# Expert weights with consecutive rows on each partition, in a two-block transformer kernel

## The chip, the cores and the metric

One NeuronCore of one Trainium2 chip runs the whole program; everything is float32 in DRAM. The metric is the device time of one execution in microseconds (us), given as the median of several runs. A profile of one execution stands beside it.

Engines are named as the profile names them: PE is the tensor engine's matmul, PEld its load of the stationary operand, DVE the vector engine, ACT the scalar engine, POOL the GpSimd engine, SP the sync engine, which here only issues DMAs. [...]

## The reference, cut to what matters

The program is two blocks of two layers each on 256 tokens of 1024 features (272 with the 16 meta tokens of block 1). The change touches only the mixture of experts that ends each layer of block 1, and a few vectors set up for it:

```python
def hier_moe(h, w_grp, b_grp, w_rtr, b_rtr, w1, w3, w2):
    t = h.reshape(-1, d)                       # [272, 1024]
    ...                                        # a group of experts, then two of its eight, and their gates
    hid = jax.nn.silu(jnp.einsum('td,edf->tef', t, w1)) * jnp.einsum('td,edf->tef', t, w3)
    y = jnp.einsum('tef,efd->td', hid * combine[..., None].astype(hid.dtype), w2)
```

There are 32 experts. `w1` and `w3` of one expert are [1024, 256], `w2` is [256, 1024]; each is 1 MB, so a layer reads 96 MB of expert weights. Each token uses two experts. `h` comes out of a layer norm with gain and bias `ln1_g`, `ln1_b`.

## The kernel before, in words

**Weights.** The contraction over 1024 features needs them on the 128 partitions in 8 blocks. The kernel puts feature `128 k + p` on partition `p` in block `k`: a weight of [1024, 256] is loaded as a tile [128, 8, 256] with `rearrange("(k p) n -> p k n")` (`moe_load`, L1109 to L1114), so that each partition receives eight separate rows of 1 KB. `w2` goes through `wrows` (L211 to L215) as [128, 2, 1024], two separate rows of 4 KB for each partition.

**Rings.** `w1` and `w3` of four experts, eight tiles `wb`, make one group; three rings hold them (5, 4 and 6 tiles: RB, RX, RC at L184), which is nearly two groups. `w2` of the four experts, tiles `w`, uses the general ring of four tiles (`wtile`, L200), which the memory projection's weights (`mem_kv`, L1595) share. All these loads are issued by SP from one queue in program order; a load waits there until its tile's last reader is done, and all loads behind it wait too.

**One group of experts** (the loop at L1253, eight groups for each of two layers): `onehot` makes a 0/1 matrix that puts each token into one of 32 slots of its expert (L1150). `gather` (L1179 to L1190) multiplies the normed tokens by it, block by block: the stationary operand is `y[t][:, k * 128:(k + 1) * 128]`, the moving one is the one-hot matrix, and the result, [128 features, 128 slots], gets the norm's gain and bias as per-partition columns of `K.lcol` (`gain`, L1171 to L1177: odd blocks on DVE, even ones on ACT) and becomes `hg[:, k, :]`. `up` (L1192) contracts `hg` with the weights, four experts side by side in four 32-column strips of the PE; tanh and two DVE products follow. `down` (L1205) transposes the hidden values by halves of 128 (L1208), multiplies by `w2` (L1216) and copies to `ysl`. `scatter` (L1221) sums the result into the token-major `acc`. Then the loads of the next group are named in program order.

A float32 matmul appears in the profile as two records, each with its own weight load. In layer 0 the tokens come in three tiles (128, 128 and 16 rows), so one gather has 8 x 3 x 2 = 48 weight loads of 128 columns; in layer 1 there are two tiles and 32 loads.

**Order of the work.** The order of instructions on each engine is set when the program is built, by a planner with costs of its own. In the first groups it puts `up(g)`, `gather(g+1)`, `down(g)`; from the fourth group on, `gather(g+1)` stands before or inside `up(g)`.

**Norm vectors.** `setup` loads `ln1_g`, `ln1_b` and other vectors as rows of 128 (L296 to L302), and `feature_columns` (L305) transposes them once into `K.lcol`, where column `16 i + 8 l + k` holds features `128 k + p`. `K.lcol` also serves the router (L674, L677) and the residual (`row_bank`, L328).

**Overflow.** `moe_overflow` (L1296) is a loop that runs only when an expert has more than 32 tokens; in the profiled execution none of its instructions stands (L1329 has no record).

Of the kernel before, what the change touches and what calls it, by code (L numbers as in the profile page):

```python
# [20 lines left out]
CAP = 32  # L21
# [19 lines left out]
def _consts():  # L41
    """Tables that depend on the shapes alone: masks, identities, rotary tables of block 1."""
# [64 lines left out]
def build(tc, A, out, dbg=None, stop=None):  # L107
    nc = tc.nc
    es = ExitStack()
    with es:  # L110
# [9 lines left out]
        # the memory's keys and values, and scratch, for the whole run  # L120
        K.pt = es.enter_context(tc.tile_pool(name="mem0", bufs=1, side="right"))
        K.mem = {0: mem_tiles(K, K.pt)}
        for l in range(2):
            with ExitStack() as st:
# [17 lines left out]
                # the expert weights start to come in beside the output projection  # L142
# [5 lines left out]
            with ExitStack() as st:  # L148
                # what dies first lies where the next phase starts
                K.pe = st.enter_context(tc.tile_pool(name="moee%d" % l, bufs=1))  # L150
                K.pf = st.enter_context(tc.tile_pool(name="moef%d" % l, bufs=1))
                K.wc = st.enter_context(tc.tile_pool(name="wringc%d" % l, bufs=RC))
                K.p = st.enter_context(tc.tile_pool(name="moe%d" % l, bufs=1))
                b1_moe(K, l)
# [12 lines left out]
        # block 2: what is needed first lies on the right, where the expert weights were  # L167
# [15 lines left out]
# tiles of the three rings of expert weights; up to which weight of a group the first two serve  # L183
# [20 lines left out]
def wcols(K, w, c0, n=256):  # L204
    """Columns c0.. of a [1024, N] weight as [128, 8, n]."""
    t = wtile(K)[:, :8 * n].rearrange("p (k n) -> p k n", n=n)
    K.nc.sync.dma_start(t, w.rearrange("(k p) n -> p k n", p=128)[:, :, c0:c0 + n])
    return t


def wrows(K, w, r0, nk=2):  # L211
    """Rows r0.. of a [K, 1024] weight as [128, nk, 1024]."""
# [5 lines left out]
def split(K, x, shape, pool=None):  # L218
    """A float32 weight block of up to 1024 columns as an exact sum of two float32r blocks."""
# [17 lines left out]
def mm3(K, out, a, b, start, stop):  # L237
    """out += a^T b to float32 accuracy; a and b are (high, low) pairs."""
# [6 lines left out]
def put(K, dst, src, sl):  # L245
    """Writes src (PSUM or SBUF) as a high and a low part."""
# [14 lines left out]
def setup(K):  # L261
# [23 lines left out]
    # the convolutions' taps as columns  # L285
# [4 lines left out]
    # a_log, dt_bias on all partitions  # L290
# [14 lines left out]
def feature_columns(K):  # L305
    """The other vectors over features as columns."""
# [5 lines left out]
    K.dng = K.const.tile([128, 2], F32, name="dng")  # L312
    V.tensor_scalar(K.dng, K.lcol[:, 64:66], 0.5, None, op0=OP.mult)


def to_T(K, src, t):
    """One token-major tile -> feature-major high and low parts."""
# [10 lines left out]
def row_bank(K, k, tag):  # L328
    """512 features from column k of K.lcol on, along a row that is the same on all partitions."""
# [6 lines left out]
def interleave(gens):  # L336
    """Runs generators in turn, one step of each, until all are done."""
# [9 lines left out]
def yield_from(gen):  # L347
    """Runs a generator to its end and gives what it returns."""
# [7 lines left out]
def b1_attention(K, l, mix, st):  # L356
# [55 lines left out]
    # small columns: db, da, iw  # L412
# [147 lines left out]
    # the memory of block 2 and the first expert weights come in early  # L560
# [13 lines left out]
def b1_sparse_meta(K, sqT, skT, vtok, mix):  # L574
    """The 16 meta tokens, all heads at once."""
# [85 lines left out]
def router_weights(K, l, p):  # L661
    """Router weights with the norm's gain on them, high and low parts; the norm's bias goes with theirs."""
# [19 lines left out]
def b1_project(K, l, mix):  # L682
    """Output projection, residual, layer norm, router logits and choices."""
# [30 lines left out]
    def norm(t, halves):  # L714
        """Residual and norm before gain and bias (left in K.y); feature-major parts of it for the router."""
# [67 lines left out]
def norm_stats(K, y, P, ss, junk, at=0):  # L783
    """Minus the mean and the inverse deviation of y [P, 1024] into ss[:, 2] and ss[:, 5]; ss[:, 0:2] holds the half sums."""
# [16 lines left out]
class Route:  # L801
    """Grouped top-2 routing, one token tile after the other: the expert slots of the tokens and their gates."""
# [26 lines left out]
    def choose(self, t):  # L829
        """The two experts of each token."""  # L830
# [18 lines left out]
    def rank(self, t):  # L849
        """The token's rank among those of the expert."""  # L850
# [9 lines left out]
    def gates(self, t):  # L860
        """Half of the gates of a token tile."""
# [16 lines left out]
class Delta:  # L878
    """Gated delta rule on one token tile: two chunks of 64, or the 16 meta tokens."""
# [12 lines left out]
    def pre(self):  # L892
# [42 lines left out]
        # normalised keys and queries, feature-major  # L935
# [33 lines left out]
        # T = (1 + L)^-1 by block doubling; U its transpose  # L969
# [37 lines left out]
        # token-major keys and values  # L1007
# [101 lines left out]
def moe_load(K, l, g, n):  # L1109
    """Weight n of a group of four experts: w1 of each, then w3 of each."""  # L1110
    t = (K.wb if n < NB else K.wx if n < NX else K.wc).tile([128, 8, 256], F32, name="wb", tag="wb")
    w = K.A["w1" if n < 4 else "w3"][l, 4 * g + n % 4]
    K.nc.sync.dma_start(t, w.rearrange("(k p) n -> p k n", p=128))
# [8 lines left out]
def b1_moe(K, l):  # L1122
    """Tokens are gathered into CAP slots per expert; tokens past the slots of an expert take a dense path in a loop
    that only runs when an expert has any."""
# [8 lines left out]
    def load(g):  # L1133
        w = [[moe_load(K, l, g, 4 * i + j) for j in range(4)] for i in range(2)]
        return w, [wrows(K, w2[4 * g + j], 0) for j in range(4)]

    # the first group's loads began beside the projection
# [4 lines left out]
    w2t = [wrows(K, w2[j], 0) for j in range(4)]  # L1142
# [4 lines left out]
    def onehot(g):  # L1147
        """Token -> slot of a group's experts."""
# [5 lines left out]
    def gates(g, oh):  # L1154
        """The gates there."""
# [4 lines left out]
    def gated(og_):  # L1160
        """Gated slot -> token."""
# [9 lines left out]
    def gain(dst, src, k):  # L1171
        """The first norm's gain and bias of feature block k."""
        g, b = (K.lcol[:, 16 * i + 8 * l + k:16 * i + 8 * l + k + 1] for i in range(2))
# [5 lines left out]
    def gather(oh):  # L1179
        hg = K.pe.tile([128, 8, 128], F32, name="hg")  # L1180
        for kk in range(2):
            ps = bank(K)
            for k in range(4 * kk, 4 * kk + 4):
                for i, t in enumerate(seq):
                    P = TP[t]
                    PE.matmul(ps[:, (k % 4) * 128:(k % 4) * 128 + 128], y[t][:P, k * 128:(k + 1) * 128],  # L1186
                              oh[:P, t, :], start=(i == 0), stop=(i == nt - 1))
# [17 lines left out]
    def down(th, w2t):  # L1205
        ps = bank(K)
        for j in range(2):
            PE.transpose(ps[:, j * 128:j * 128 + 128], th[:, j * 128:j * 128 + 128], ident)  # L1208
# [29 lines left out]
    # the meta tokens' sums lie beside them  # L1238
# [3 lines left out]
    def init():  # L1242
        """The residual, of the normed tokens."""
# [30 lines left out]
    # tokens without a slot  # L1274
# [21 lines left out]
def moe_overflow(K, l, ovf, acc, rows, tiles, gain):  # L1296
    """Adds the contribution of the tokens that found no slot, whatever their number."""
# [3 lines left out]
    with tc.If(n > 0):  # L1301
        # tokens feature-major, and the gates of those past the slots
        yT = [K.wx.tile([128, 8, TP[t]], F32, name="yT%d" % t, tag="wb") for t in tiles]
        for t in tiles:
            P = TP[t]
            for b in range(2):
                ps = bank(K)
                for j in range(4):
                    k = 4 * b + j
                    PE.transpose(ps[:, j * P:(j + 1) * P], K.y[t][:P, k * 128:(k + 1) * 128], c["ident"][:P, :P])  # L1310
# [3 lines left out]
        with tc.For_i(0, 32, 1) as e:  # L1314
            def cols(w):
                t = wtile(K).rearrange("p (k n) -> p k n", n=256)
                nc.sync.dma_start(t, w[l, bass.ds(e, 1)].rearrange("o (k p) n -> p (o k) n", p=128))
# [3 lines left out]
            nc.sync.dma_start(w2t, A["w2"][l, bass.ds(e, 1)].rearrange("o (k p) n -> p (o k) n", p=128))  # L1321
            for t in tiles:
# [13 lines left out]
                for j in range(2):  # L1336
                    PE.transpose(ps[:, j * 128:j * 128 + P], th[:P, j * 128:j * 128 + 128], c["ident"][:P, :P])
# [10 lines left out]
def setup2(K):  # L1348
    """Per-feature vectors of block 2."""
# [30 lines left out]
def setup2_rest(K):  # L1380
    """Masks, gains on token-major heads, and rotary tables."""
# [10 lines left out]
    # cos and sin of positions * inv, with the multiples of 2 pi taken off exactly  # L1392
# [29 lines left out]
def rms_T(K, src, gain, dst):  # L1422
    """RMS norm of two token-major tiles, feature-major as high and low parts [128, 8, 256]; gain is columns [128, 8]."""
# [23 lines left out]
def rstd_heads(K, ss, P, n, d):  # L1447
    """(ss / d + 1e-6) ** -0.5 on [P, n]."""
# [25 lines left out]
def weave(a, b, na, nb):  # L1474
    """Runs generator a beside b: nb steps of b for every na of a."""
    done = [False, False]
    i = 0
# [776 lines left out]
```

## Time and profile before

| | |
|---|---|
| median of 3 runs | 2196.48 us (2181.83 to 2199.58) |
| span of the profiled execution, first to last instruction | 2178.1 us |
| mean granted PE clock | 0.954 |
| PE busy | 2037.9 us, 94% of the span |
| DMA traffic from HBM | 411.5 MB, 190 GB/s on average |
| expert stage of layer 0 | about 316 to 585 us |
| expert stage of layer 1 | about 886 to 1139 us |

The span is that of one execution of its own, and each run is timed from outside; the runs lie 4 to 21 us above this span. A busy PE is not a PE at its peak, since the ends of its matmuls are modelled. The stages are read from the first gather matmul to the last scatter matmul of each layer.

### The profile page before, as it was taken

How to read it: one execution, taken by the hardware profiler on the slowest of the kernel's cores; microseconds unless marked ns; L12 is line 12 of the kernel's file. 1: busy time of each engine (PE TensorE's matmuls, PEld its weight loads, DVE VectorE, ACT ScalarE, POOL GpSimd, SP SyncE). 2: the span in 40 equal slices, each digit the busy share in tenths (PEclk: the TensorE clock that was granted, in tenths of full speed). 3: DMA queues.
4: the chain of work that ended last, by engine and by line, in shares of the span. 5: the costliest groups of instructions: out<-in, count | busy, mean ns of one | idle time of the engine just before them, and what ended most of it. 6: DMA issues, size and time to landing. Idle time of an engine off the chain costs nothing. (4 is left out here: it accounts for less than half of the span.)

```text
span 2178.1 us, 34809 instructions
## 1 busy us (share of the span) xinstructions
PE 2037.9 (94%) x14216; PEld 1588.2 (73%) x14216; DVE 1091.5 (50%) x2179; ACT 762.0 (35%) x1478; POOL 358.9 (16%) x342
## 2 busy tenths in 40 slices
PE   8999999999699999988768999999999999999999
PEld 7888665544299887543326779889878869898987
DVE  6658444221376583521116674555545575555554
ACT  5214322111242243211015434455534524445543
POOL 1325000000022430000001130123400031122410
PEclk9999799999899997999889899999999989999999
DMA  7304288999942154999995243254555434244553
GB/s 220 97 20 136 78 290 297 340 356 371 301 132 74 44 187 141 344 368 366 365 335 170 83 166 120 88 184 155 173 194 163 133 116 146 88 153 145 168 193 116
DMA packets 321670, 414.90 MB, mean 190 GB/s; under 512 B 25480, under 2 KB 277970, under 8 KB 321506
## 3 DMA queue, kind: packets, MB, share of 16 engines
q1 hardware_dynamic: 315110, 410.85, 56.4%
q8 instruction: 114, 1.87, 0.4%
q10 hardware_dynamic: 6396, 1.77, 0.3%
q14 instruction: 50, 0.41, 0.1%
HBM read 411.54 MB, written 1.05 MB: 189 GB/s over the span
## 5 line engine op out<-in xcount | busy, mean ns | idle before, releaser
L233 DVE TENSOR_TENSOR wl<-w,wh 128x1024 fp32r<-128x1024 f32 x329 | 411.5, 1253 | 270.8 <-ACT wh L232 263.5
L232 ACT CAST wh<-w 128x1024 fp32r<-128x1024 f32 x350 | 365.7, 1047 | 429.8 <-PE ps_d L241 251.3
L240 PE MATMUL ps_d<-hh,wh 128*128 128x256 f32 (+1 forms) x1632 | 481.7, 296 | 5.5 <-ACT tg L2161 1.9
L242 PE MATMUL ps_d<-hh,wl 128*128 128x256 f32 (+1 forms) x1632 | 475.1, 291 | 0.3
L241 PE MATMUL ps_d<-hl,wh 128*128 128x256 f32 (+1 forms) x1632 | 475.0, 291 | 0.0
L240 PEld LDWEIGHTS ps_d<-hh,wh 128*128 128x128 f32 x1632 | 310.1, 190 | 17.4 <-issue 6.4
L242 PEld LDWEIGHTS ps_d<-hh,wl 128*128 128x128 f32 x1632 | 310.6, 190 | 9.1 <-DVE wl L233 6.9
L241 PEld LDWEIGHTS ps_d<-hl,wh 128*128 128x128 f32 x1632 | 310.1, 190 | 4.7 <-issue 0.8
L1197 PE MATMUL ps_d<-wb,hg 128*32 128x256 f32 x2048 | 156.0, 408 | 33.1 <-DMA wb<-in_w 33.0
L1197 PEld LDWEIGHTS ps_d<-wb,hg 128*32 128x32 f32 x2048 | 73.4, 117 | 106.5 <-DMA wb<-in_w 43.4
L2221 POOL TENSOR_TENSOR relu<-relu 128x256 f32<-128x256 f32 x64 | 86.6, 1354 | 129.6 <-ACT relu L2220 129.6
L1186 PE MATMUL ps_c<-oh,y 128*128 128x128 f32 (+1 forms) x640 | 101.9, 297 | 0.0
L1201 DVE SCALAR_TENSOR_TENSOR mth<-mth,ps_d 128x256 f32<-128x256 f32 x16 | 6.7, 421 | 183.5 <-ACT mth L1200 183.4
L1186 PEld LDWEIGHTS ps_c<-oh,y 128*128 128x128 f32 (+1 forms) x640 | 82.7, 189 | 21.1 <-issue 5.7
L1216 PE MATMUL ps_d<-w,hid 128*32 128x512 f32 x512 | 80.9, 637 | 12.1 <-ACT hid L1210 7.9
L795 POOL TENSOR_TENSOR lnst<-lnst,nhalf 128x1 f32<-128x1 f32 (+1 forms) x5 | 4.9, 980 | 479.7 <-DVE lnst L794 477.8
L1228 DVE TENSOR_TENSOR yacc<-yacc,ps_c 128x512 f32<-128x512 f32 x56 | 38.5, 687 | 83.6 <-PE ps_c L1225 83.6
L1200 ACT ACTIVATE mth<-ps_d 128x256 f32<-128x256 f32 x16 | 6.1, 383 | 211.5 <-PE ps_d L1197 211.5
L233 POOL TENSOR_TENSOR wl<-w,wh 128x1024 fp32r<-128x1024 f32 x21 | 50.0, 2383 | 129.2 <-ACT wh L232 119.8
L2175 POOL TENSOR_TENSOR mergedT<-mergedT,tg 128x256 f32<-128x256 f32 x32 | 32.6, 1041 | 234.0 <-DVE tg L2173 234.0
L1216 PEld LDWEIGHTS ps_d<-w,hid 128*32 128x32 f32 x512 | 21.7, 115 | 60.3 <-issue 36.8
L1225 PE MATMUL ps_c<-ysl,ohT 128*128 128x512 f32 (+1 forms) x140 | 64.5, 603 | 0.0
(679 smaller groups left out, 3686.1 us busy)
## 6 DMA issues: line engine op xcount, KB each, us to landing
wb<-in_w SPq DMA_DIRECT2D x128, 1024.0 KB, 12.0
w<-in_w_in SPq DMA_DIRECT2D x82, 1024.0 KB, 5.3
w<-in_w SPq DMA_DIRECT2D x64, 1024.0 KB, 11.4
w<-in_w_up SPq DMA_DIRECT2D x32, 1024.0 KB, 5.3
w<-in_w_down SPq DMA_DIRECT2D x32, 1024.0 KB, 4.9
w<-in_w_out SPq DMA_DIRECT2D x16, 1024.0 KB, 4.8
w<-in_w_branch SPq DMA_DIRECT2D x24, 512.0 KB, 4.2
w<-in_mem_w_kv SPq DMA_DIRECT2D x8, 1024.0 KB, 5.7
```

The source lines that it names most:

```text
L232: K.nc.scalar.copy(h, x)
L233: eng.tensor_tensor(lo, x, h.bitcast(F32), op=OP.subtract)
L240: PE.matmul(out, a[0], b[0], start=start, stop=False, skip_group_check=True)
L241: PE.matmul(out, a[0], b[1], start=False, stop=False, skip_group_check=True)
L242: return PE.matmul(out, a[1], b[0], start=False, stop=stop, skip_group_check=True)
L1186: PE.matmul(ps[:, (k % 4) * 128:(k % 4) * 128 + 128], y[t][:P, k * 128:(k + 1) * 128], oh[:P, t, :], start=(i == 0), stop=(i == nt - 1))
L1197: PE.matmul(pu[j * 32:j * 32 + 32, i * 256:i * 256 + 256], hg[:, k, j * 32:j * 32 + 32], wts[i][j][:, k, :], start=(k == 0 and i == 0), st ...
L1216: PE.matmul(ps[q * 32:q * 32 + 32, :], hid[:, j, q * 32:q * 32 + 32], w2t[q][:, j, hf * 512:(hf + 1) * 512], start=(j == 0), stop=(j == 1) ...
L1225: PE.matmul(ps[rows[t]], ohT[:, off:off + P], ysl[:, hf * 512:(hf + 1) * 512], start=True, stop=True)
L1228: V.tensor_tensor(sl, sl, ps[rows[t]], op=OP.add)
L2175: G.tensor_tensor(m, m, tg, op=OP.add)
L2221: G.tensor_tensor(r, r, r, op=OP.mult)
```

## The change

The expert weights are loaded so that a partition holds consecutive rows: features `8 p + k` for `w1` and `w3`, hidden features `2 p + j` for `w2`. The rest follows that order: `gather` takes every eighth column of the token tile as its stationary operand, the transposes in `down` every second column of the hidden values, and the norm's gain and bias come from a new tile `K.gcol` that is loaded by two DMAs on ACT's queue. The residual and the router keep `K.lcol`. The overflow loop is changed the same way. The diff also removes comments and docstrings, which are left out here.

```diff
 def feature_columns(K):
...
     K.dng = K.const.tile([128, 2], F32, name="dng")
+    K.gcol = K.const.tile([128, 2, 2, 8], F32, name="gcol")
+    for i, nm in enumerate(("ln1_g", "ln1_b")):
+        K.nc.scalar.dma_start(K.gcol[:, i], K.A[nm].rearrange("l (p k) -> p l k", k=8))
     V.tensor_scalar(K.dng, K.lcol[:, 64:66], 0.5, None, op0=OP.mult)
...
 def moe_load(K, l, g, n):
     t = (K.wb if n < NB else K.wx if n < NX else K.wc).tile([128, 8, 256], F32, name="wb", tag="wb")
     w = K.A["w1" if n < 4 else "w3"][l, 4 * g + n % 4]
-    K.nc.sync.dma_start(t, w.rearrange("(k p) n -> p k n", p=128))
+    K.nc.sync.dma_start(t, w.rearrange("(p k) n -> p k n", k=8))
+    return t
+
+
+def moe_load2(K, w):
+    t = wtile(K).rearrange("p (k n) -> p k n", n=1024)
+    K.nc.sync.dma_start(t, w.rearrange("(p k) n -> p k n", k=2))
     return t
...
-        return w, [wrows(K, w2[4 * g + j], 0) for j in range(4)]
+        return w, [moe_load2(K, w2[4 * g + j]) for j in range(4)]
...
-    w2t = [wrows(K, w2[j], 0) for j in range(4)]
+    w2t = [moe_load2(K, w2[j]) for j in range(4)]
...
     def gain(dst, src, k):
-        g, b = (K.lcol[:, 16 * i + 8 * l + k:16 * i + 8 * l + k + 1] for i in range(2))
+        g, b = (K.gcol[:, i, l, k:k + 1] for i in range(2))
...
-                    PE.matmul(ps[:, (k % 4) * 128:(k % 4) * 128 + 128], y[t][:P, k * 128:(k + 1) * 128],
-                              oh[:P, t, :], start=(i == 0), stop=(i == nt - 1))
+                    PE.matmul(ps[:, (k % 4) * 128:(k % 4) * 128 + 128], y[t][:P, k::8], oh[:P, t, :], start=(i == 0), stop=(i == nt - 1))
...
-            PE.transpose(ps[:, j * 128:j * 128 + 128], th[:, j * 128:j * 128 + 128], ident)
+            PE.transpose(ps[:, j * 128:j * 128 + 128], th[:, j::2], ident)
```

## Rows read from the trace of the kernel before

**Rows 1.** The page: busy time and instructions of each engine, then 40 equal slices.
```profile
PE 2037.9 (94%) x14216; PEld 1588.2 (73%) x14216; DVE 1091.5 (50%) x2179; ACT 762.0 (35%) x1478; POOL 358.9 (16%) x342
...
GB/s 220 97 20 136 78 290 297 340 356 371 301 132 74 44 187 141 344 368 366 365 335 170 83 166 120 88 184 155 173 194 163 133 116 146 88 153 145 168 193 116
```

**Rows 2.** Windows in the expert stages: first from:to and length; then stretches of one load kind.
```profile
core 0: us, PE busy (x) PEld busy (x) DVE busy (x) ACT busy (x) POOL busy (x), PEclk, DMA share, GB/s
480.00:536.00 56.00, 52.88 (x416) 27.84 (x416) 12.00 (x22) 5.74 (x14) 0.00 (x0) 0.97 1.08 366
536.00:580.00 44.00, 32.90 (x216) 11.19 (x216) 6.88 (x15) 4.77 (x11) 0.00 (x0) 0.88 0.99 344
...
1085.00:1131.00 46.00, 32.28 (x243) 12.57 (x247) 6.05 (x14) 4.57 (x11) 0.00 (x0) 0.80 1.06 375
395.00:410.00 15.00, 14.41 (x78) 6.88 (x78) 5.61 (x11) 3.26 (x7) 0.00 (x0) 1.00 1.10 348
1120.00:1130.00 10.00, 7.47 (x65) 3.31 (x68) 1.16 (x4) 0.76 (x2) 0.00 (x0) 0.67 1.03 409
```

**Rows 3.** DMA packets in 395 to 410, then in 1120 to 1130.
```profile
DMA packets 5177, 5.22 MB, mean 348 GB/s; under 512 B 80, under 2 KB 5177, under 8 KB 5177
...
DMA packets 1068, 4.09 MB, mean 409 GB/s; under 512 B 69, under 2 KB 69, under 8 KB 1068
```

**Rows 4.** Waits of PE in 316 to 580, in 886 to 1131, in 886 to 1019.
```profile
PE ps_d L1197 <- DMA wb<-in_w: 7.7, 4, 2.4
...
PE ps_d L1197 <- DMA wb<-in_w: 25.3, 13, 2.5
...
PE ps_d L1216 <- DMA w<-in_w: 3.5, 5, 0.9
...
PE ps_d L1197 <- DMA wb<-in_w: 4.4, 2, 2.4
...
PE ps_d L1216 <- DMA w<-in_w: 1.6, 2, 0.9
```

**Rows 5.** Timeline of PE: start, length, line, operation, count, idle time before.
```profile
355.52 0.62 PE L1197 MATMUL ps_d<-wb,hg 128*32 128x256 f32 x2
...
382.05 0.62 PE L1197 MATMUL ps_d<-wb,hg 128*32 128x256 f32 x2
...
553.55 3.65 PE L1197 MATMUL ps_d<-wb,hg 128*32 128x256 f32 x60 [1.07 <-DMA wb<-in_w]
...
565.58 5.92 PE L1197 MATMUL ps_d<-wb,hg 128*32 128x256 f32 x58 [1.93 <-DMA wb<-in_w]
...
904.76 3.74 PE L1186 MATMUL ps_c<-oh,y 128*128 128x128 f32 x32
```

**Rows 6.** Weight loads of the gather and of `up`: ns min/median/max, first and last start.
```profile
L1186 PEld LDWEIGHTS ps_c<-oh,y x640: 181/192/192, 316.2 to 1074.0; 128*128 128x128 f32 x128, 16*128 16x128 f32 x32
...
L1197 PEld LDWEIGHTS ps_d<-wb,hg x2048: 106/110/178, 325.2 to 1126.7; 128*32 128x32 f32 x187
```

**Rows 7.** Two DVE lines of block 2, the same view: ns min/median/max.
```profile
L1914 DVE TENSOR_TENSOR raw<-R,fcol x8: 569/598/1580, 1226.9 to 1746.4; 128x240 f32<-128x240 f32 x8
...
L1797 DVE TENSOR_TENSOR garg<-G x12: 407/418/428, 1230.1 to 1763.7; 128x256 f32<-128x256 f32 x12
```

**Rows 8.** SP in layer 1: its timeline, a wait of it, and loads issued from 1019 on.
```profile
1007.88 11.10 SPq L214 DMA_DIRECT2D w<-in_w  x4
...
SPq L214 <- PE ps_p L1600: 6.3, 1, 6.3
...
wb<-in_w SPq DMA_DIRECT2D x24, 1024.0 KB, 12.0
w<-in_w SPq DMA_DIRECT2D x12, 1024.0 KB, 14.4
```

**Rows 9.** DMA in 1152.2 to 1160: packets, and one of the loads.
```profile
DMA packets 2591, 1.71 MB, mean 219 GB/s; under 512 B 1695, under 2 KB 2032, under 8 KB 2590
...
qkg<-in_nsa_k_norm SPq DMA_DIRECT2D x2, 96.0 KB
```

More of the change, by code (lines that the diff above doesn't have):

```diff
@@ L1309, in moe_overflow @@
                     k = 4 * b + j
-                    PE.transpose(ps[:, j * P:(j + 1) * P], K.y[t][:P, k * 128:(k + 1) * 128], c["ident"][:P, :P])
+                    PE.transpose(ps[:, j * P:(j + 1) * P], K.y[t][:P, k::8], c["ident"][:P, :P])
                 for j in range(4):
@@ L1316, in cols @@
                 t = wtile(K).rearrange("p (k n) -> p k n", n=256)
-                nc.sync.dma_start(t, w[l, bass.ds(e, 1)].rearrange("o (k p) n -> p (o k) n", p=128))
+                nc.sync.dma_start(t, w[l, bass.ds(e, 1)].rearrange("o (p k) n -> p (o k) n", k=8))
                 return t
@@ L1320, in moe_overflow @@
             w2t = wtile(K).rearrange("p (k n) -> p k n", n=1024)
-            nc.sync.dma_start(w2t, A["w2"][l, bass.ds(e, 1)].rearrange("o (k p) n -> p (o k) n", p=128))
+            nc.sync.dma_start(w2t, A["w2"][l, bass.ds(e, 1)].rearrange("o (p k) n -> p (o k) n", k=2))
             for t in tiles:
@@ L1336, in moe_overflow @@
                 for j in range(2):
-                    PE.transpose(ps[:, j * 128:j * 128 + P], th[:P, j * 128:j * 128 + 128], c["ident"][:P, :P])
+                    PE.transpose(ps[:, j * 128:j * 128 + P], th[:P, j::2], c["ident"][:P, :P])
                 hid = K.pe.tile([128, 2, 128], F32, name="hid")
```

## The prediction, made before the changed kernel was run

> **What bounds the kernel now.** I read the page first. PE is busy for 94% of the span, but the share of busy time is a mean, and the slices of GB/s show two stretches, about 270 to 600 us and 870 to 1140 us, in which the traffic stays between 290 and 371 GB/s while elsewhere it is mostly under 200 [rows 1]. They are the two expert stages. Nothing outside them is changed, so the next view is the windows inside them: the DMA engines' share is 0.99 to 1.08, so they have no free time, and PE is busy for 52.88 of 56 us in 480 to 536, but only for 32.9 of 44 us in 536 to 580 and for 32.28 of 46 us in 1085 to 1131 [rows 2]. Both resources are close to the bound, PE ahead in layer 0 and DMA in layer 1. PE's waits say by how much: in layer 0's stage PE waits 7.7 us for `wb`; in layer 1's it waits 25.3 + 3.5 = 28.8 us for expert weights, 4.4 + 1.6 = 6.0 us of them before 1019 [rows 4]. All that a faster load can give back is in these waits and in the slow clock behind them.
>
> **The loads.** In a stretch with `w1`/`w3` alone DMA moves 348 GB/s, with `w2` alone 409 [rows 2]; the packets are 1 KB in the first (5.22 MB in about 5,100) and 4 KB in the second (4.09 MB in about 1,000 over 2 KB), one for each row on each partition [rows 3]. One MB (1.0486e6 bytes) takes 3.01 us in the one form and 2.56 us in the other. The difference, 0.45 us for 768 packets less on 16 engines, is 9.4 ns a packet. With 8 KB on a partition the packets fall from 256 to 128, so 2.56 - 8 x 0.0094 = 2.49 us, some 421 GB/s; no row shows packets of 8 KB, and the bounds are 2.56 (no faster than 4 KB) and 2.49. I take 2.49: 0.52 us less for a `w1`/`w3` tile, 0.07 for a `w2` tile, so 8 x 0.52 + 4 x 0.07 = 4.4 us for a group, 71 us for all 16, if all of it were on the path. That the two inner dimensions are joined to one run is shown by a load elsewhere: the `qkg` rows, written in the program as 3 x 64 elements, move 96 KB to 128 partitions; in their window 2032 - 1695 = 337 packets have between 512 B and 2 KB [rows 9], where only 768 B rows and one load with 128 rows of 512 B can stand.
>
> [...]
>
> **The gather's weight loads.** This is the price. The stationary operand becomes `y[:, k::8]`, one float32 in every 32 bytes. The trace has no stationary operand with such a step, so I bound it. A load of 128 columns lasts 192 ns, one of 32 columns 110 ns [rows 6]: 82 ns for 96 columns, 0.85 ns a column, 109 ns for the 128. In layer 1 a gather's 32 loads with their matmuls take 3.74 us, 117 ns each [rows 5], so loads are about as long as what they hide behind, and a longer load shows in full. The lower bound is no extra at all: a gain is excluded, since the same columns pass either way. For the upper side the nearest rows are two on DVE. L1914 reads float32 at the same step of 32 bytes: 569 ns at best for 240 elements; L1797 reads 256 elements at a step of 8 bytes or less in 418 ns [rows 7]. At about 1 ns an element 240 would take 401, so the step costs 168 ns, 0.70 ns an element (by the median, 197 ns or 0.82). For 128 columns that is 90 to 105 ns, close to a doubled load (109). I take 100 ns a load, being nearest to the only rows with this step; the ends kept for the range are 0 and, for a load four times as long, 327.
>
> [...]
>
> In numbers: 8 gathers x 48 loads x 0.1 = 38.4 us in layer 0 and 8 x 32 x 0.1 = 25.6 us in layer 1.
>
> **What of it is on the path.** Layer 0: between 355.52 and 382.05 one group takes 26.5 us on PE [rows 5], with no DMA wait, and until about 536 PE is the one that is late. So the 38.4 us lie on PE's chain. Given back are the 7.7 us of waits for `wb` and the slow clock after them: 58 matmuls of `up` took 5.92 us behind the waits against 3.65 for 60 [rows 5], 2.3 us. After that DMA has slack, since its group takes 12 x 2.49 = 30 us against PE's 26.5 + 4.8 = 31.3. Layer 0: 38.4 - 10.0 = +28.4.
>
> Layer 1: SP's queue is held at 1007.88 for 11.10 us, 6.3 of them by the memory projection's matmuls on PE, which occupy two of the four `w` tiles; behind this stand 24 `wb` and 12 `w` loads [rows 8], which are DMA's path to the end of the stage. The hold moves with PE: six gathers lie before it, 6 x 3.2 = 19.2 us, less the 6.0 us of waits. Behind it the loads are faster by 24 x 0.52 + 12 x 0.07 = 13.3 us. Sum 19.2 - 6.0 - 13.3 = -0.1; the two gathers after it (6.4 us) fit into the 22.8 - 13.3 = 9.5 us of waits that are left. Layer 1: 0. What is late next there is PE and DMA alike.
>
> The rest I cost at nothing. The transposes' loads are 32 in all at a step of 8 bytes, which L1797 reads without a loss; were each doubled it would be about 3 us. `K.gcol` adds two small DMAs on ACT's queue, issued with the constants some 250 us before the first gather; ACT is busy 35% of the span, and its issue delays nothing that PE waits for then. SP's queue gets no more entries than before.
>
> **Sum.** +28.4 - 0.1 = +28, less a little for a planner that may put the gather back behind `up`, where the wait for tanh is covered: +27 us on a span of 2178.1. Set on the median of the runs, 2196.5, that is **2223.5 us**, 1.2% slower.
>
> **The rivals.**
> (B) *Strided loads cost PE nothing.* Then layer 0 keeps the -10.0 and layer 1 has -6.0 - 13.3 = -19.3 and some 3 us of slow clock (0.80 granted in 1085 to 1131, between the two levels [rows 2]). Sum -32: 2164 us, 1.5% faster. For it: a PE load takes 0.85 ns a column, slower than its matmuls stream, and its read path need not be DVE's. Against it: rows 7. It decides below 20 ns a load, where faster loads outweigh what is left.
> (C) *The strided load takes four times as long*, 327 ns more for 640 loads: 209 us, less some 39 given back: 2366 us. Nothing in the trace speaks for it, but nothing shows the step on PE.
> (D) *The runs are not joined, or 8 KB runs are no faster* than what is there. Then only the price is left: 38.4 - 10.0 and, in layer 1, 19.2 - 6.0 = 13 before the hold: 2238 us. Against it: rows 9 and the step from 348 to 409.
> (E) *A price in between* (about 50 ns a load): 14 - 10 in layer 0 and -6 - 13 + 10 in layer 1, some -4: 2192 us.
>
> **How the numbers follow.** Chances: forecast 0.52, B 0.33, C 0.06, D 0.06, E 0.03. The forecast's own range is +10 to +42: below if the planner moves the gathers or the price is 85 ns, above if it is 109 or the waits come back elsewhere. The whole range goes from B's better half (2152) to the forecast's upper end (2240); left out are C, a part of D and the tails, about 0.17. About 1% (22 us) is what a measurement can tell from no change. Faster by more: B, 0.33. Slower by more: 0.6 of the forecast (0.31), C and two thirds of D, 0.41. Within 1%: 0.26.
>
> **What would show it.** Right: the weight loads of the gather's line near 290 ns where they were 192, a gather of layer 1 in about 7 us for 3.74; packets of 8 KB, and over 410 GB/s in stretches with `wb` alone; PE's waits for `wb` in layer 0 gone, its stage about 28 us longer, layer 1's as long as before. Wrong: loads at 192 ns with layer 1's stage 20 us shorter (B), packets of 1 KB (D), or an order of `up` and gather that differs from before by more than the loads explain.

## The result, and the profile after

The changed kernel takes 2252.44 us (2244.98 to 2266.49, 4 runs), the kernel before in the same measurement 2191.97 us; the ratio is 1.029, 95% interval 1.024 to 1.034. The forecast said slower, 2223.5 us; the measured time lies 12 us above the upper end of its range. The direction is that of the forecast, and so is the first cause, the strided weight load. The size is not: 60 us for 27. A second cause, a fall of PE's granted clock in layer 0's stage (0.97 before, 0.79 after), stood in no term of the sum.

The page of the changed kernel, with the rows that answer to [rows 1], and the granted clock in the same 40 slices:
```profile
PE 2156.3 (95%) x14216; PEld 1697.3 (75%) x14216; DVE 1092.4 (48%) x2179; ACT 761.7 (34%) x1478; POOL 358.9 (16%) x342
...
PEclk9999598678789997799998989999999989999999
...
GB/s 217 88 30 165 30 279 238 266 234 357 272 291 86 57 100 143 189 334 351 354 424 261 133 123 135 88 145 149 171 195 175 140 112 139 85 142 153 173 191 114
```
The number of PE instructions is the same, but PE is busy for 118 us more and PEld for 109 us more. The granted clock is a share of full speed; every clock record of these two traces is 1.00 or 0.50, the upper and the lower level of what follows, and a figure between them is a mean over a window. In the first expert stage (slices 7 to 12) the granted clock is at 0.6 to 0.8, where [rows 2] had 0.88 to 1.00, and the traffic lies between 234 and 357 GB/s: DMA waits there for PE to free its tiles (in layer 0's stage SP waits 126 us for the matmuls of `up`, 38 us before). One slice of layer 1's stage shows 424 GB/s.

The weight loads of the gather (line 1198, line 1186 before) and of `up` (line 1208), to be held against [rows 6]: ns min/median/max.
```profile
L1198 PEld LDWEIGHTS ps_c<-oh,y x640: 307/334/340, 327.9 to 1163.7; 128*128 128x128 f32 x128, 16*128 16x128 f32 x32
...
L1208 PEld LDWEIGHTS ps_d<-wb,hg x2048: 106/110/178, 344.1 to 1201.1; 128*32 128x32 f32 x187
```
The load of the gather went from 192 to 334 ns; the load of `up`, which was not touched, is at 110 ns as before.

The timeline of PE, first in layer 0, then in layer 1, as in [rows 5]:
```profile
410.51 5.77 PE L1227 MATMUL ps_d<-w,hid 128*32 128x512 f32 x32 [0.46 <-ACT hid L1221]
...
429.11 16.22 PE L1198 MATMUL ps_c<-oh,y 128*128 128x128 f32 x48
...
1011.09 7.78 PE L1198 MATMUL ps_c<-oh,y 128*128 128x128 f32 x32
...
1019.68 3.64 PE L1227 MATMUL ps_d<-w,hid 128*32 128x512 f32 x32 [0.59 <-ACT hid L1221]
```
A gather of layer 1 takes 7.78 us for 3.74. One of layer 0 takes 16.22; before, the same 48 matmuls stood in one row of the timeline with 8.71 us. The first row is a product with `w2` that stands about 1 us behind the gather before that one: 5.77 us, where the same 32 matmuls take 3.64 in layer 1; the granted clock of this stretch was 0.62.

The windows of a gather, the first row from the kernel before (391 to 400, layer 0):
```profile
391.29:399.92 8.63, 8.63 (x50) 6.69 (x50) 2.22 (x5) 1.30 (x3) 0.00 (x0) 1.00 1.10 349
```
and from the changed kernel, two in layer 0, one in layer 1, then a stretch of 33 us with expert weights alone:
```profile
429.11:445.08 15.97, 15.97 (x49) 12.71 (x49) 2.22 (x5) 1.30 (x3) 0.00 (x0) 0.59 1.01 423
562.13:570.32 8.19, 8.19 (x25) 6.35 (x24) 0.00 (x0) 0.00 (x0) 0.00 (x0) 0.50 0.46 192
1011.09:1018.67 7.58, 7.58 (x34) 7.58 (x33) 1.88 (x5) 1.84 (x4) 0.00 (x0) 1.00 1.01 426
1127.00:1160.00 33.00, 30.84 (x221) 19.78 (x221) 5.64 (x12) 4.13 (x10) 0.00 (x0) 0.95 1.01 424
```
The DMA view of that stretch, as in [rows 3]:
```profile
DMA packets 1923, 13.98 MB, mean 424 GB/s; under 512 B 219, under 2 KB 219, under 8 KB 219
```
The columns after the length are the busy times of PE, PEld, DVE, ACT and POOL, then the granted clock. Read PEld against the length. In layer 1 a load is under way all the time (7.58 of 7.58). In layer 0 it is so for 12.71 of 15.97 us; the other 3.26 us are the 16 places in a gather where the operand changes between 128 and 16 rows, 0.20 us each on average. Before, this gap was (8.63 - 6.69) / 16 = 0.12 us. The clock is the other difference: 1.00 in layer 1 and before, 0.59 and 0.50 in the changed kernel's layer 0.

The two differences are one. The fifth gather of layer 0 stands in two pieces, at two levels of the clock:
```profile
457.56:463.12 5.56, 5.56 (x19) 4.78 (x18) 0.56 (x1) 0.39 (x1) 0.00 (x0) 0.96 1.01 423
464.29:473.73 9.44, 9.44 (x29) 7.37 (x28) 0.00 (x0) 0.00 (x0) 0.00 (x0) 0.50 0.10 42
```
The first has 6 changes of rows and 0.78 us without a load, 0.13 us each; the second 9 and 2.07 us, 0.23 each. Read load by load over all of layer 0's gathers, the pause at a change is 0.12 us wherever the clock is at its upper level (34 of them here, 126 in the kernel before) and 0.22 us wherever it is at the lower one (91). A strided load of 128 rows itself takes 335 ns at either level. So the step lengthens the loads, and the low clock lengthens the pauses between them.

How much of the stage runs at the lower level is told by the granted clock over layer 0's stage, 0.97 before and 0.79 after:
```profile
316.65:584.86 268.21, 248.25 (x1869) 126.48 (x1868) 70.79 (x158) 36.36 (x87) 2.03 (x2) 0.97 0.98 336
328.36:652.31 323.95, 312.69 (x1869) 177.76 (x1868) 70.83 (x158) 36.61 (x87) 2.03 (x2) 0.79 0.68 275
```
That is 17 us of 268 at the lower level before, and 133 of 324 after.

The last of the four windows above and the packets are what the longer runs give: 1923 - 219 = 1,704 packets of 8 KB, 424 GB/s, where there were 348 with 1 KB packets [rows 2].

PE's waits in layer 0's stage, then in layer 1's, as in [rows 4]:
```profile
PE ps_d L1227 <- DMA w<-in_w: 0.3, 1, 0.3
...
PE ps_d L1208 <- DMA wb<-in_w: 5.8, 4, 1.9
...
PE ps_d L1227 <- DMA w<-in_w: 0.5, 1, 0.5
```
The 7.7 us of waits for `wb` in layer 0 are gone (no row is left), the 28.8 us of layer 1 are 6.3.

Where the time came from is told by adding, for each line, the time from the start of a matmul to the start of the next one (so waits and the clock are in it), over each stage from its first gather to its last scatter (differences are taken before rounding):

| us, before -> after | layer 0 | layer 1 |
|---|---|---|
| stage | 268.2 -> 324.0, +55.8 | 252.6 -> 247.6, -5.0 |
| gather | 69.3 -> 128.0, +58.8 | 30.1 -> 62.4, +32.3 |
| `up` with its waits | 87.3 -> 83.0, -4.3 | 115.5 -> 83.5, -32.0 |
| `down`'s product with `w2` | 38.9 -> 36.8, -2.1 | 45.2 -> 40.9, -4.3 |
| memory projection beside it (42 matmuls in layer 0) | 18.6 -> 21.1, +2.5 | 19.6 -> 19.6, 0.0 |

The stages give 55.8 - 5.0 = +51 us. The two profiled executions differ by 36 us more outside the stages, where nothing was changed. The profile of after is that of its slowest run. The time outside the stages (span less both stages) is 1693 us there and 1657 before; in the profiles below it is 1648 to 1680. It goes with the clock: 229 us of it are at the lower level after and 150 before, and over all 14 profiles of this case each further us at the lower level comes with 0.44 us more (correlation 0.99). Why the clock differs there from run to run is not shown. Medians of runs differ by 60 us, so some 10 us are not placed by the stages.

### The profile page after: what moved, and what is told of

It is laid out like the page before. It is cut to its first block, busy times and chain, and to the rows that moved or that the text cites. A ratio compares the mean times of both kernels' runs of the same rounds, so it can differ in the third digit from the quotient of the medians.

```text
span 2264.7 us, 34811 instructions
## 1 busy us (share of the span) xinstructions
PE 2156.3 (95%) x14216; PEld 1697.3 (75%) x14216; DVE 1092.4 (48%) x2179; ACT 761.7 (34%) x1478; POOL 358.9 (16%) x342
## 5 line engine op out<-in xcount | busy, mean ns | idle before, releaser
L1198 PE MATMUL ps_c<-oh,y 128*128 128x128 f32 (+1 forms) x640 | 193.2, 451 | 0.0
L1198 PEld LDWEIGHTS ps_c<-oh,y 128*128 128x128 f32 (+1 forms) x640 | 163.6, 329 | 31.4 <-issue 26.8
L1208 PE MATMUL ps_d<-wb,hg 128*32 128x256 f32 x2048 | 147.0, 402 | 5.8 <-DMA wb<-in_w 5.8
L1227 PEld LDWEIGHTS ps_d<-w,hid 128*32 128x32 f32 x512 | 21.7, 125 | 52.4 <-issue 38.4
```

Of the source, the lines that this page charges most:

```text
L1208: PE.matmul(pu[j * 32:j * 32 + 32, i * 256:i * 256 + 256], hg[:, k, j * 32:j * 32 + 32], wts[i][j][:, k, :], start=(k == 0 and i == 0), st ...
L1227: PE.matmul(ps[q * 32:q * 32 + 32, :], hid[:, j, q * 32:q * 32 + 32], w2t[q][:, j, hf * 512:(hf + 1) * 512], start=(j == 0), stop=(j == 1) ...
```

## The experiments

Theory 1 is that the strided weight load of the gather is the whole price, and that the loads alone gain what the prediction's rival B said. Rival 1: a part of the loss comes from the new tile of norm vectors or the order that the program gets from it. Rival 2: the larger packets gain nothing on the path.

**One part alone.** The first run strides the gather and keeps the loads; the second keeps the new loads and takes the stride away.

In both, weights and tokens stand in different orders of features, so the results are of no use; the number of instructions on each engine is that of the kernel before.

The stride alone, on the kernel before:

```diff
-  y[t][:P, k * 128:(k + 1) * 128]
+  y[t][:P, k::8]
```

The loads alone, on the changed kernel:

```diff
-  y[t][:P, k::8]
+  y[t][:P, k * 128:(k + 1) * 128]
```

The norm tile alone, in the old order, on the kernel before:

```diff
+    K.gcol = K.const.tile([128, 2, 2, 8], F32, name="gcol")
+    for i, nm in enumerate(("ln1_g", "ln1_b")):
+        K.nc.scalar.dma_start(K.gcol[:, i], K.A[nm].rearrange("l (k p) -> p l k", p=128))
...
-        g, b = (K.lcol[:, 16 * i + 8 * l + k:16 * i + 8 * l + k + 1] for i in range(2))
+        g, b = (K.gcol[:, i, l, k:k + 1] for i in range(2))
```

> The kernel before, with only the gather's stationary operand changed to every eighth column; the loads stay as before, so the order of features in the gathered tokens does not match that of the weights. Theory 1 (the price is the strided weight load): the gather's loads last 334 ns as in the changed kernel, a gather of layer 1 takes 7.7 to 7.9 us for 3.74, one of layer 0 about 16 for 8.71, together +91 us of PE; given back are only waits that PE's lateness covers (7.7 us in layer 0, about 6 in layer 1 before SP's hold, and a part of the 22.8 behind it), so the time is 2255 to 2280 us, ratio 1.03 to 1.04, more than the changed kernel's 1.029. Rival 1 (half of the loss comes from the new order of the program or from the small tile of norm vectors): ratio 1.01 to 1.02. The granted clock tells a third thing: if it falls below 0.9 in layer 0's expert stage, where it was 0.96 to 1.00, the fall belongs to the strided loads.

> The changed kernel, with the gather's stationary operand put back to contiguous columns; it has the 8 KB packets, the new norm tile and the transposes over every second column, and the order of features in the gathered tokens does not match that of the weights. Theory 1: gather back at 3.7 and 8.7 us, PE's waits for w1/w3 fall from 33 us to under 10, layer 0's clock at 0.95 or more; 2155 to 2170 us, ratio 0.98 to 0.99 (the prediction's rival B). Rival 2 (bigger packets gain nothing on the path, DMA is hidden anyway): ratio 0.995 to 1.005. Rival 1 (the order or the norm tile costs by itself): above 1.005.

> The kernel before, with only the norm's gain and bias moved to a tile of their own, loaded by two small DMAs on ACT's queue in the old feature order. Theory 1: ratio 0.997 to 1.003. Rival 1 (these DMAs or the order that the planner makes of them delay the program ahead of the first gather, which starts 12 us later in the changed kernel): ratio 1.005 to 1.015 and a first gather at 322 us or later.

| | ratio to before (95%) | stage of layer 0, 1 (us) | gather, layer 0, 1 (us) |
|---|---|---|---|
| kernel before | 1 | 268.2, 252.6 | 8.66, 3.76 |
| changed kernel | 1.029 (1.024 to 1.034) | 324.0, 247.6 | 16.01, 7.81 |
| stride alone | 1.038 (1.030 to 1.046) | 328.6, 261.6 | 15.96, 7.81 |
| loads alone | 0.987 (0.979 to 0.996) | 253.3, 226.0 | 8.66, 3.76 |
| norm tile alone | 1.002 (0.998 to 1.007) | 266.0, 250.1 | 8.66, 3.76 |

(In this and the later tables a gather is the sum of its line, from start to start, over eight.) The loads of the gather with the stride alone and with the loads alone:
```profile
L1186 PEld LDWEIGHTS ps_c<-oh,y x640: 307/334/338, 321.8 to 1155.8; 128*128 128x128 f32 x128, 16*128 16x128 f32 x32
```
```profile
L1198 PEld LDWEIGHTS ps_c<-oh,y x640: 181/192/193, 319.1 to 1047.1; 128*128 128x128 f32 x128, 16*128 16x128 f32 x32
```
The stride alone is slower than the whole change, the loads alone are faster than before, and the norm tile cannot be told from nothing: theory 1 holds if what the clock does is counted with the strided load, and rivals 1 and 2 fall. The late first gather of the changed kernel (328 us for 316) is no effect of the norm tile: with that tile the ratio stays at 1.002, though in its profile the first gather starts at 332. Both go with the clock ahead of it: 34 us at the lower level in the kernel before, 58 in the changed one, 65 with the norm tile alone. With the stride alone the gathers of layer 0 run at the same low clock (0.59 to 0.68 in the first four), and with the loads alone at 1.00, so the fall of the clock comes with the strided gather and not with the new loads.

Taking the stride out of the changed kernel shortens layer 0's stage by 70.7 us. The loads are 8 x 48 x 0.125 = 48 us of it. The other 22 are what goes with the clock (0.99 in that stage for 0.79): some 10 us of pauses in the gathers, 8 us of `up` without its waits (75.2 us for 67.2), and the rest in the memory projection and the product with `w2`.

**How the price goes with the step.** Two, four and eight consecutive rows give packets of 2, 4 and 8 KB and a gather over every second, fourth and eighth column.

Four rows, on the changed kernel; the norm tile and the overflow loop follow, and the kernel with two rows has 2 in place of 4 and 256 of 512:

```diff
+def feat(k):
+    a, b = divmod(k, 4)
+    return slice(512 * a + b, 512 * (a + 1), 4)
...
-    K.nc.sync.dma_start(t, w.rearrange("(p k) n -> p k n", k=8))
+    K.nc.sync.dma_start(t.rearrange("p (a b) n -> p a b n", b=4), w.rearrange("(a p b) n -> p a b n", p=128, b=4))
...
-  y[t][:P, k::8]
+  y[t][:P, feat(k)]
```

Every step in one gather, on the changed kernel:

```diff
-  y[t][:P, k::8]
+  y[t][:P, 0:128 * (k + 1):k + 1]
```

> w1 and w3 with four consecutive rows on a partition (packets of 4 KB, 409 GB/s by the trace of before), the gather over every fourth column, a step of 16 bytes. If only a step beyond 16 bytes is paid for: loads at 192 ns, gather of layer 1 at 3.7 us, 2160 to 2180 us, ratio 0.985 to 0.995. If every step that leaves adjacent elements is paid in full: loads at 334 ns, 2245 to 2265 us, ratio 1.025 to 1.035. If the price grows with the step: loads at 220 to 300 ns and a ratio in between, 1.00 to 1.02. The transposes over every second column, whose loads took 217 ns for 141, speak for a price at 8 bytes already.

> w1 and w3 with two consecutive rows on a partition (packets of 2 KB, 84 ns each by the trace of before, some 390 GB/s), the gather over every second column, a step of 8 bytes. At 16 bytes a load took 329 ns, at 32 bytes 334, contiguous 192. If any step costs the same: 320 to 334 ns, gather of layer 1 at 7.6 us. If the price depends on the bytes between two elements: about 240 ns or less, a gather of layer 1 under 5.5 us. If 8 bytes are free: 192 ns and 3.8 us. The transposes at this step took 217 for 141.

> The changed kernel, with block k of the gather over columns at a step of k + 1 elements, so that one gather holds every step from 4 to 32 bytes side by side; the features gathered are not those of the weights. Read in layer 1's first gather, where nothing interrupts it: four loads for each step. The steps of 8, 16 and 32 bytes gave 196, 329 and 334 ns. If the price begins where two elements no longer lie in the same 16 bytes: about 192 to 200 ns at 4 and 8 bytes, something between at 12 (two of four neighbours still share 16 bytes), 325 to 335 from 16 bytes on, 20 and 28 included. If it belongs to powers of two (16 and 32 bytes alone): 12, 20, 24 and 28 bytes stay near 200.

Four rows: 1.032 (1.025 to 1.040), as slow as eight. Two rows: 0.988 (0.978 to 0.998, two runs), faster than the kernel before, with stages of 260.5 and 233.3 us. The loads, by four rows and by two:
```profile
L1204 PEld LDWEIGHTS ps_c<-oh,y x640: 302/329/333, 319.5 to 1144.9; 128*128 128x128 f32 x128, 16*128 16x128 f32 x32
```
```profile
L1204 PEld LDWEIGHTS ps_c<-oh,y x640: 187/196/198, 321.3 to 1065.2; 128*128 128x128 f32 x128, 16*128 16x128 f32 x32
```
And the dial, in layer 1's first gather: four loads for each step, from 4 bytes in the first row, 4 bytes more in each, to 32 bytes in the last:
```profile
L1198 PEld LDWEIGHTS ps_c<-oh,y x4: 186/190/192, 936.4 to 936.8; 128*128 128x128 f32 x4
...
L1198 PEld LDWEIGHTS ps_c<-oh,y x4: 196/196/197, 936.9 to 937.2; 128*128 128x128 f32 x4
...
L1198 PEld LDWEIGHTS ps_c<-oh,y x4: 254/261/263, 937.3 to 937.9; 128*128 128x128 f32 x4
...
L1198 PEld LDWEIGHTS ps_c<-oh,y x4: 318/330/330, 938.0 to 938.7; 128*128 128x128 f32 x4
...
L1198 PEld LDWEIGHTS ps_c<-oh,y x4: 319/321/321, 939.0 to 939.6; 128*128 128x128 f32 x4
...
L1198 PEld LDWEIGHTS ps_c<-oh,y x4: 318/318/318, 939.9 to 940.5; 128*128 128x128 f32 x4
...
L1198 PEld LDWEIGHTS ps_c<-oh,y x4: 323/326/326, 940.8 to 941.4; 128*128 128x128 f32 x4
...
L1198 PEld LDWEIGHTS ps_c<-oh,y x4: 334/334/336, 941.7 to 942.4; 128*128 128x128 f32 x4
```
So in a gather 8 bytes cost 6 ns over 190, 12 bytes half of the full price (71 of 140 ns), and from 16 bytes on the price is full and flat (318 to 334 ns); powers of two play no part, since 20, 24 and 28 bytes are at 321, 318 and 326 ns. From 8 to 12 bytes a load is 65 ns longer, from 12 to 16 bytes another 69. These are the times of the first of the two expectations; what in the load makes them so, no run shows.

**The changes of rows.** The gather's loop is turned: the tile of 16 tokens comes once in each half of the features instead of once in each block.

On the changed kernel, and in the same way on the kernel before:

```diff
-            for k in range(4 * kk, 4 * kk + 4):
-                for i, t in enumerate(seq):
-                    P = TP[t]
-                    PE.matmul(ps[:, (k % 4) * 128:(k % 4) * 128 + 128], y[t][:P, k::8], oh[:P, t, :], start=(i == 0), stop=(i == nt - 1))
+            for i, t in enumerate(sorted(seq, key=lambda t: (t == 2, -t))):
+                P = TP[t]
+                for k in range(4):
+                    PE.matmul(ps[:, k * 128:k * 128 + 128], y[t][:P, 4 * kk + k::8], oh[:P, t, :], start=(i == 0 and k == 0), stop=(i == nt - 1),
+                              skip_group_check=True)
```

> The changed kernel, with the gather's loop turned: within a half of the features first the two tiles of 128 tokens for four blocks, then the tile of 16 tokens for four blocks, so that a gather of layer 0 changes between 128 and 16 rows 4 times and not 32. In the changed kernel a strided load follows its like after 238 ns, and after 370 at a change of rows. If the changes of rows make layer 0's gathers so much longer than layer 1's: 48 x 0.24 + 4 x 0.13 = 12 us for 16.0, layer 0's stage some 30 us shorter, layer 1 unchanged, ratio to the kernel before 1.010 to 1.020. If the granted clock of 0.55 to 0.65 in layer 0's gathers belongs to these changes, it is 0.9 or more now, as in layer 1's; if it belongs to the strided loads of a 16-row tile or to the stage, it stays under 0.75.

> The kernel before with the gather's loop turned alone. A gather of layer 0 in 6.2 us for 8.66 (as with the permuted copy), 20 us less of PE in layer 0; there a group's loads take 8 x 3.01 + 4 x 2.56 = 34.3 us of DMA, so most of it comes back as waits for w1/w3: 0 to 10 us shorter, ratio 0.994 to 1.001. If the turned loop alone carried the gain of the run with copy and turned loop (0.980): 0.985 or less.

The changed kernel with the loop turned: ratio 1.010 (1.003 to 1.018), layer 0's stage 296.4 us for 324.0, its gather 12.40 for 16.01, layer 1's stage 247.8 as before the turn. Two numbers of the expectation are put right here: there are 16 changes in a gather, not 32, and by the starts in the trace two loads stand 0.56 us apart across a change at the lower clock and 0.45 at the upper one (0.31 in the kernel before), not 0.37. The sum comes out alike, 44 x 0.238 + 4 x 0.45 to 0.56 = 12.3 to 12.7. The windows of two of these gathers:
```profile
408.94:421.10 12.16, 12.16 (x49) 11.70 (x48) 2.22 (x5) 1.30 (x3) 0.00 (x0) 0.86 1.01 425
563.78:569.91 6.13, 6.13 (x25) 5.85 (x24) 0.00 (x0) 0.00 (x0) 0.00 (x0) 0.50 1.01 428
```
The pauses without a load are 0.46 us of 12.16. The clock came back in part: 0.86 for 0.59, but 0.50 for 0.50 in the second half of a late gather. So the turn takes back half of the loss in layer 0 (27.6 of 55.8 us), and the changes of rows account for a part of the low clock only. The 16-row loads are as many as before the turn, and layer 1, which has none, stays at 1.00; whether they hold the clock down in the rest stays open.

On the kernel before, the turned loop gives 0.994 (0.990 to 0.998): 20 us less of PE in layer 0, of which waits for `wb` take back 5 (12.7 us for 7.7), and a stage 10.2 us shorter, the upper end of what was expected.

**Versions without the price.** The tokens are copied once for each layer into the order of the gather, and the gather reads the copy contiguously. The residual starts in place, which frees the room for the copy.

On the changed kernel (the tile of 16 tokens goes through two scratch tiles, left out here):

```diff
+    yp = K.yp = [K.pf.tile([128, 1024], F32, name="yp%d" % t) if t < 2 else y[2] for t in tiles]
+    for t in seq:
+        dst = yp[t][:TP[t]].rearrange("p (k q) -> p k q", q=128)
+        if t < 2:
+            S.copy(dst, y[t][:].rearrange("p (q k) -> p k q", k=8))
...
-  y[t][:P, k::8]
+  yp[t][:P, k * 128:(k + 1) * 128]
...
-    acc = [K.pf.tile([128, 1024], F32, name="yacc%d" % t) if t < 2 else y[2][rows[2]] for t in tiles]
+    acc = [y[t] if t < 2 else y[2][rows[2]] for t in tiles]
```

> The changed kernel, with the normed tokens copied once for each layer into the order of the gather (tile 0 and 1 by ACT, the 16-row tile by way of two small scratch tiles), and the gather over contiguous columns of the copy; the residual is started in place. Theory 1 (the strided loads are the whole price): gathers back at 8.7 and 3.8 us, 2150 to 2170 us, ratio 0.985 to 0.993, that is the run with contiguous columns (0.987) plus 0 to 5 us for the copies ahead of the first gather. If the copies lie on the path to the first gather: up to 3 x 2.5 us in each layer, ratio 0.993 to 0.998. If the loads' gain depended on the wrong order of features: 1.0 or more.

> As the run with the permuted copy, and the gather's loop turned as well. A gather of layer 0 falls from 8.7 to 48 x 0.109 + 4 x 0.1 = 5.7 us, 24 us less of PE in layer 0; there a group's loads take 30 us of DMA against PE's 28, so a part comes back as waits for w1/w3: layer 0's stage 5 to 20 us shorter than with the copy alone, ratio 0.976 to 0.988. If DMA bounds layer 0 already with the copy alone: equal to it within 3 us.

> The run with two consecutive rows and a step of 8 bytes, with the gather's loop turned as well; no copy is needed. Gather of layer 0 in about 6.4 us for 8.97. Packets of 2 KB: 8 x 2.7 + 4 x 2.5 = 31.6 us of DMA for a group, 8 of them 253 us, against a stage of 260 us in layer 0: 5 to 12 us shorter, ratio 0.980 to 0.988; slower than the copy with 8 KB packets (0.980) by 5 to 15 us.

| | ratio to before (95%) | stage of layer 0, 1 (us) | gather, layer 0, 1 (us) |
|---|---|---|---|
| permuted copy | 0.986 (0.979 to 0.994) | 254.7, 226.9 | 8.80, 3.76 |
| permuted copy, loop turned | 0.980 (0.973 to 0.987) | 240.5, 225.9 | 6.18, 3.76 |
| two rows, loop turned | 0.984 (0.978 to 0.990) | 245.8, 234.5 | 6.48, 3.96 |
| kernel before, loop turned | 0.994 (0.990 to 0.998) | 258.0, 250.7 | 6.18, 3.76 |

The copies of the two tiles of 128 tokens in layer 0, on ACT, in the version with the copy alone:
```profile
L1247 ACT COPY yp<-y 128x1024 f32<-128x1024 f32 x2 | 4.1, 2047 | 2.1 <-DVE rk L862 2.1
```
They take 2.05 us each, and the second ends at 316.3, before the first gather's first load at 317.8. With the turned loop a gather of layer 0 takes 6.18 us, not the 5.7 of the expectation. The copy with the turned loop is the fastest kernel here: 2137.59 us, 2.0% under the kernel before and some 5% under the changed one. Two rows with the turned loop need no copy; their interval overlaps with it, so which of the two is better is not settled.

**`w2` alone.**

On the kernel before:

```diff
-        return w, [wrows(K, w2[4 * g + j], 0) for j in range(4)]
+        return w, [moe_load2(K, w2[4 * g + j]) for j in range(4)]
...
-            PE.transpose(ps[:, j * 128:j * 128 + 128], th[:, j * 128:j * 128 + 128], ident)
+            PE.transpose(ps[:, j * 128:j * 128 + 128], th[:, j::2], ident)
```

> The kernel before, with only w2's two rows on a partition made consecutive (8 KB packets for 4 KB) and the transposes over every second column. By the prediction's term 0.07 us a tile, 4.5 us in all if DMA were on the path everywhere; by the trace of the changed kernel 1.2 us more for the transposes; ratio 0.996 to 1.002, no difference that can be told. If w2's form carried a good part of the 1.3% that the loads give: 0.994 or less.

Ratio 0.999 (0.995 to 1.003): no difference that can be told; the form of `w2` gives half a percent at most by itself, so most of the 1.3% that the loads give is `w1` and `w3`.

The weight loads of the transposes, before and in this run, all at a clock of 1.00:
```profile
L1208 PEld LDWEIGHTS ps_c<-cst,mth x32: 137/141/144, 347.2 to 1128.7; 128*128 128x128 f32 x32
...
L1214 PEld LDWEIGHTS ps_c<-cst,mth x32: 194/201/219, 353.8 to 1130.3; 128*128 128x128 f32 x32
```
Here the step of 8 bytes costs 60 ns, where it cost 6 in the gather. The difference lies in the contiguous load: the same 128 columns take 141 ns in the transposes, which come in twos, and 190 in the unbroken row of a gather. So 8 bytes are nearly free only where the load is that long already; why it is, no run shows.

## Why the prediction was wrong in size

**What held.** PE is the late one in layer 0, DMA's gain goes unused there (SP's waits for the matmuls of `up` went from 38 us to 126), and the strided load is the price: the run with the stride alone (1.038) and that with the loads alone (0.987) show both halves by themselves. The loads were sized well: 421 GB/s forecast, 424 measured; 8 KB packets (rival D falls); PE's waits for `wb` in layer 0 gone. Rival B, free strided loads, was priced at -32 us; with the stride taken away the stages give 14.9 + 26.6 = -41.5 us, the medians 1.3% or -28.

**The step that failed** is the price of the gather in layer 0, "8 gathers x 48 loads x 0.1 = 38.4 us". It came to 58.8. Two things are in the 20 us. First, the load costs 0.125 us more, not 0.100: (12.71 - 6.69) / 48, and in layer 1 (7.81 - 3.76) / 32 = 0.127. This is 8 x 48 x 0.025 = 9.6 us. The estimate was taken from DVE rows with the same step [rows 7]; another engine's row gave the right order of size and no more. Second, the sum took a gather's price to be its loads alone, at a clock that stays as it was. The clock fell to the lower level in most of layer 0's gathers, and there each pause at a change of rows is 0.22 us for 0.12: by the gather shown, (3.26 - 1.94) x 8 = 10.6 us. That the pauses exist could be read in the trace of before: 8.71 us for 48 loads is 181 ns a load, where layer 1 has 117. That the clock would fall could not: there these gathers run at 1.00.

**The next term that failed** is the return in layer 0, "38.4 - 10.0", for the same reason. The waits were given back, 7.7 us, but not the 2.3 us of slow clock behind them; instead there is a new stretch at the low clock, 133 us of the stage for 17. `up` without its waits takes 75.2 us for 71.7, and the memory projection 2.5 us more, together some 6 us lost where 2.3 were to be gained. With 20.4 + 8.3 us, less 2.1 that the product with `w2` gained and 0.8 more for the transposes, the +28.4 of layer 0 become the 55.8 measured. As an estimate from these rows, a third of the missing 27 us is the size of the load and the rest is the clock, which the prediction counted as a small gain. What brings the clock down is shown in part only: strided loads together with the 16-row tile, since it stays at 1.00 with contiguous columns and in layer 1, and fewer changes of rows bring some of it back (0.86 for 0.59 in the gather shown).

**Layer 1** was forecast at 0 and came to -5.0, by the chain that the prediction named. The hold of SP's queue, before the same 24 `wb` and 12 `w` loads [rows 8], is now
```profile
1083.89 27.18 SPq L1125 DMA_DIRECT2D w<-in_w  x4
```
It ends 145.4 us after the stage's first gather, 132.2 before: +13.2 us, where 19.2 - 6.0 = 13.2 was forecast. From there to the last scatter it is 102.2 us for 120.4, -18.2 where -13.3 was forecast. That the first agrees so well is luck: the six gathers cost 24.3 us more, not 19.2, and 11 us came back before the hold, not 6.0. Over the whole stage the price is 32.3 us for 25.6 and the return 36.3 for 19.3; of the return 22.5 us are waits, and 12.6 are `up` without its waits (67.8 us for 80.4), in a stage whose granted clock rose from 0.93 to 0.96.

**The signs in the trace** went beyond what the forecast named: 334 ns for "near 290", 7.78 us for "about 7", +55.8 for "+28". The transposes at 8 bytes were costed at nothing and cost 1.2 us in all. Rival E's sum does not follow from its own price: 50 ns a load are 19 us in layer 0, not 14. What stays open are the 10 us between the stages (+51) and the medians (+60, interval 52 to 75); the time outside the stages varies by some 30 us, with the clock, among profiles whose code is the same there.

## What to carry to other kernels

A layout that gives DMA longer runs moves the step into whoever reads the other operand: look up who reads it, how often, and at what step in bytes, before the packets are counted. Here 8 bytes (two float32) were nearly free for the gather's weight loads (196 ns for 190) and 16 were not (330), so two rows for each partition, or one copy into the new order (two copies of 2 us on ACT, done before the first gather), give the gain without the price. Where an instruction stands in an unbroken row in one place and between others of another shape elsewhere, take its price from both places, and look what rows at the lower clock say of it.

## What the runs showed that was not expected

- A gather's strided weight load is priced in steps: 190, 196, 261, 330 ns at 4, 8, 12, 16 bytes, and 318 to 334 from there to 32. In the transposes, where a contiguous load takes 141 ns, 8 bytes cost 60.
- A change between 128 and 16 rows is a pause without a load: 0.12 us at the upper clock, with strided loads as with contiguous ones, and 0.22 us at the lower clock. Turning the loop, with no other change, made the kernel before 0.6% faster.
- In layer 0's strided gathers PE was counted as busy all the time, and the granted clock fell to between 0.50 and 0.75 in most of them; in layer 1's, with loads just as long (335 ns) but no pause between them, it stayed at 1.00.
